# A hybrid mLSTM, attention and MoE layer: keys weighted on ScalarE as they leave PSUM, gate columns as bias of the exponential, late output transposes, wider adaLN sums

## The chip, the cores and the metric

The kernel runs on one core of a Trainium2 chip, in one launch. The metric is the device time of an execution in microseconds. Engines: PE is TensorE, DVE VectorE, ACT ScalarE, POOL GpSimd, SP the engine whose queue issues most DMAs.

## The reference, cut to what matters

One layer on 1024 tokens of width 1024, all in float32. The part that the change touches is the modulation (adaLN) and the mLSTM mixer with four heads of width 128, run forward and backward over the sequence. After it come dilated attention, the output projection and an expert-choice MoE with 16 experts, which the change leaves as they are.

```python
mod = jax.nn.silu(c) @ w_ada[l] + b_ada[l]          # 6 x 1024 numbers
shift1, scale1, gate1, shift2, scale2, gate2 = jnp.split(mod[:, None, :], 6, axis=-1)
h = rms_norm(x, norm1_g[l]) * (1.0 + scale1) + shift1
proj = h @ w_in[l]
x_m, o_pre, i_fw, f_fw, i_bw, f_bw, a_q, a_k, a_v = jnp.split(proj, split_points, axis=-1)
...
# mlstm_chunkwise, per head and direction (the kernel uses chunks of 128):
    w = jnp.exp(ac - m_new[..., None])               # weight of each key
    C_new = decay * C + einsum('bhl,bhld,bhle->bhde', w, kc, vc)
...
D = where(lower, b[..., :, None] - b[..., None, :] + i_pre[..., None, :], -inf)
w_intra = exp(D - m_t[..., None]) * einsum('bhcte,bhcje->bhctj', q, k)
num = w_inter[..., None] * einsum('bhcte,bhced->bhctd', q, C_prev) + einsum('bhctj,bhcjd->bhctd', w_intra, v)
h = num / maximum(abs(den), exp(-m_t))[..., None]
...
h = h_fwd + h_bwd
h = h * rsqrt(mean(h * h, -1) + 1e-6) * out_norm_g + skip * xc
```

## The kernel before, in words

The kernel is written in a tile language: Python says which instructions each part issues, and a list scheduler sorts them, by its own estimates, into one fixed order for each engine before anything runs. On the chip each engine follows its list and waits at an instruction until what it needs is there. The order views below are such lists.

The change lies in one stage, in which `body` interleaves three streams (`interleave((proj_stream, 1.0), (mlstm_stream, 1.9), (ada_stream, 1.0))`); the numbers that the streams yield are their estimated share of PE time, and steer in what order their work is handed to the scheduler.

- `proj_stream` computes the attention's q, k and v: 24 blocks of 128 tokens, 8 k-slabs and 3 products of 128x512 for each (lines L388, L389, L390), into the four PSUM buffers `pa`. ACT rounds each weight slab (`wh`, L345), DVE takes the rest (`wl`, L346), and DVE and ACT in turn move the results out (`ev`, L395, L397).
- `mlstm_stream` handles the gates first (`mlstm_gates`: scans over rows, which at L504 to L516 are transposed by PE, L513, into the columns `gcol`, or written to DRAM as `gate_rows_d`), then four heads one after another. A head: q by a product with a block diagonal matrix (L542, moved out by ACT, L543); the keys transposed (L552, moved out as `k` by ACT, L553); v (L557, L558); for each direction d the weights `W`, loaded as gate rows repeated over 128 partitions (POOL's DMA, L564), masked by POOL (L565), gate column added by DVE (L566), exponential by ACT (L567); `qw` loaded (L570) and multiplied with q (L573), its last columns copied by POOL as `dec` (L572); `kw`, the keys times a gate column, by POOL (L577). Then q·k on PE in two groups of four 128x128 (L583), multiplied into W by DVE (L586). Eight steps follow, each for both directions: state products (L600), intra-chunk and inter-chunk products (L605, L607), the state update on DVE (L613, L615), the denominators (L618 to L620) and the output (L624 on ACT, L626 on DVE). At the head's end the sum of squares (L629, L631), the inverse root (`rsqrt`, L134 to L139), the norm (L634), two groups of four transposes (L639), and the update of `og` (L641). The convolution of the next head (L523, L525) is issued within the head.
- `ada_stream` forms the upper 4096 numbers of `mod`: in 16 blocks of 256 columns, `w_ada` times silu(c) is summed on DVE over eight slabs (L319, L321 in `ada_sum`; SP's DMAs bring two slabs of 128x256 at once), then PE adds the 128 partitions with products by ones (L981), and DVE adds the bias (L982).

The last two streams share the four PSUM buffers `pb`. The tiles W, qw, kw and xc have two buffers each, q, k, v and h one; the square of L629 takes one of W's.

Of the kernel before, what the change touches and what calls it, by code (L numbers as in the profile page):

```python
# [20 lines left out]
P = 128  # L21
S = 1024
# [88 lines left out]
class K:  # L111
# [342 lines left out]
    def mlstm_gates(self):  # L454
# [30 lines left out]
        ch = lambda x: x.rearrange("p (c t) -> p c t", t=P)  # L485
        r_, c_, em, ws, wi = t, R("k"), R("q"), R("xc"), R("v")
        nc.vector.tensor_sub(r_, b_, m_)
# [41 lines left out]
    def mlstm_stream(self):  # L529
# [4 lines left out]
        self.mlstm_gates()  # L534
        yield 2.0
        for h in range(MH):
            xc, xm = xcs[h], self.xm[h]

            q = T("q")
            for b in range(2):  # L540
                ps = self.psB.tile([P, 512], F32, name="pb")
                nc.tensor.matmul(ps, self.amat[:, h, :], xc[:, b * 512:(b + 1) * 512], start=True, stop=True)  # L542
                nc.scalar.activation(q[:, b * 512:(b + 1) * 512], ps, AF.Copy)  # L543
            k = T("k", [P, NT, P])
            v = T("v", [P, NT, E1])
            nc.gpsimd.memset(v[:, :, P:E1], 1.0)
            yield 1.7
            for b in range(2):
                ps = self.psB.tile([P, 4, P], F32, name="pb")
                for i in range(4):  # L550
                    t = slice((4 * b + i) * P, (4 * b + i + 1) * P)
                    nc.tensor.transpose(ps[:, i, :], xc[:, t], self.ident)  # L552
                nc.scalar.activation(k[:, 4 * b:4 * b + 4, :], ps, AF.Copy)  # L553
                ps = self.psB.tile([P, 4, P], F32, name="pb")
                for i in range(4):
                    t0 = 2 + (4 * b + i) * P
                    nc.tensor.matmul(ps[:, i, :], xm[:, t0:t0 + P], self.bdv[:, h, :], start=True, stop=True)  # L557
                nc.scalar.activation(v[:, 4 * b:4 * b + 4, 0:P], ps, AF.Copy)  # L558
                yield 1.3

            W, QW_, KW, DEC = [], [], [], []
            for d in range(2):
                z = T("W", [P, NT, P])
                nc.gpsimd.dma_start(out=z, in_=bc(self.rows_d[0, d, h:h + 1, :], P))  # L564
                nc.gpsimd.tensor_add(z, z, self.mask[:, d:d + 1, :].to_broadcast([P, NT, P]))  # L565
                nc.vector.tensor_add(z, z, self.gcol[:, 0, :, MH * d + h][:, :, None].to_broadcast([P, NT, P]))  # L566
                nc.scalar.activation(z, z, AF.Exp)  # L567
                W.append(z)
                wi = T("qw")
                nc.gpsimd.dma_start(out=wi, in_=bc(self.rows_d[1, d, h:h + 1, :], P))  # L570
                dec = cw.tile([P, NT], F32, name="dec", bufs=4)
                nc.gpsimd.tensor_copy(dec, wi[:, P - 1:S:P] if d == 0 else wi[:, 0:S:P])  # L572
                nc.vector.tensor_mul(wi, wi, q)  # L573
                QW_.append(wi)
                DEC.append(dec)
                kw = T("kw", [P, NT, P])
                nc.gpsimd.tensor_mul(kw, k, self.gcol[:, 2, :, MH * d + h][:, :, None].to_broadcast([P, NT, P]))  # L577
                KW.append(kw)
            for b in range(2):
# [4 lines left out]
                for d in range(2):  # L584
                    w = W[d][:, 4 * b:4 * b + 4, :]
                    nc.vector.tensor_mul(w, w, ps)  # L586
                yield 0.9
            if h + 1 < MH:
                xcs[h + 1] = self.mlstm_conv(h + 1)
# [45 lines left out]
            yield 0.1  # L635
            for b in range(2):
                ps = self.psB.tile([P, 4, P], F32, name="pb")
                for i in range(4):
                    nc.tensor.transpose(ps[:, i, :], h_[:, 4 * b + i, :], self.ident)  # L639
                t = slice(b * 512, (b + 1) * 512)  # L640
                nc.vector.scalar_tensor_tensor(og[:, t], ps.rearrange("p a b -> p (a b)"), self.vcol("mlstm_norm_g", h), og[:, t], op0=OP.mult, op1=OP.add)  # L641
            yield 0.9

# [322 lines left out]
    def ada_stream(self):  # L966

        nc = self.nc
        wada = self.I["w_ada"].rearrange("(p k) n -> p k n", k=KT)
        for q in range(2 * KT):  # L970
            c = (KT + q) * 256
            acc = self.cw.tile([P, 256], F32, name="ada_acc2")
            for k in range(0, KT, 2):
                aw = self.cw.tile([P, 2, 256], F32, name="ada_w2", bufs=3)
                nc.sync.dma_start(out=aw, in_=wada[:, k:k + 2, c:c + 256])
                yield 0
                self.ada_sum(acc, aw, k)
                yield 1.5
            ps = self.psB.tile([P, 512], F32, name="pb")
            for j in range(2):  # L980
                nc.tensor.matmul(ps[:, j:j + 1], acc[:, j * P:(j + 1) * P], self.ones[:, 0:1], start=True, stop=True)  # L981
            nc.vector.tensor_add(self.modc[:, 2 * q:2 * q + 2], ps[:, 0:2], self.vcol("b_ada", 2 * KT + 2 * q, 2))  # L982
            yield 0.5

# [618 lines left out]
def body(tc, I, out):  # L1603
    with ExitStack() as ctx:
# [13 lines left out]
        k.cw = k.pool("mlstm_work", st_cw, side="right")  # L1618
        k.tags = dict(W=2, qw=2, kw=2, q=1, k=1, v=1, h=1, xc=2)
        interleave((k.proj_stream(), 1.0), (k.mlstm_stream(), 1.9), (k.ada_stream(), 1.0))  # L1620
# [81 lines left out]
```

## Time and profile before

| what | us |
|---|---|
| median of 3 runs | 1914.62 |
| the runs | 1909.89, 1918.05, 1914.62 |
| the profiled execution | 1909.63 |
| its span, first to last instruction | 1907.9 |
| mean granted PE clock over the span | 0.973 of full speed |

The profile comes from one execution. An engine is busy while an instruction runs; what ended an idle time is the wait that is named. A matmul with float32 operands shows as two instructions. "PEclk" is the clock that PE was granted, as a share of the full one. In the 40 slices of the span the stage described above is the third to the eighth: PE reads 9 8 9 8 9 8 there, POOL 1 3 2 1 2 1, the clock 9 8 9 9 9 9.

```profile
PE   6998989889998939999999999999999999999997
...
DVE  6778887668775787877877877877776777867765
ACT  4343231358774436766766765756766666666654
POOL 1313212122122000000100100100000001000000
PEclk9998999999999968999999999999999999999999
```

### The profile page before, as it was taken

Reading aid. Unit: us, or ns where it says so; the run is one execution under the profiler, and the core shown is the slowest. Engines: PE = TensorE matmul, PEld = TensorE weight load, DVE = VectorE, ACT = ScalarE, POOL = GpSimd, SP = SyncE. Lnnn points to the kernel's source line nnn. Section 1 sums busy time; section 2 is a strip of 40 time slices with the busy share of each in tenths; the row PEclk is TensorE's granted clock in tenths of the full one; section 3 lists DMA queues with packets and bytes.
Section 4 is the critical chain, followed back from the end, with each engine's and each line's share of the span. In section 5 each row is a group of like instructions: output and inputs, shape, how many; then the busy total and the mean of one; then the engine's idle time right before and its main releaser. Section 6 shows DMA issues by size and latency. Waiting matters only on the chain. (4 is left out here: it accounts for less than half of the span.)

```text
span 1907.9 us, 23733 instructions
## 1 busy us (share of the span) xinstructions
PE 1780.7 (93%) x8457; PEld 1383.5 (73%) x8457; DVE 1436.8 (75%) x2218; ACT 1096.5 (57%) x1429; POOL 221.5 (12%) x200
## 2 busy tenths in 40 slices
PE   6998989889998939999999999999999999999997
PEld 4677777778887837777777777776776777777775
DVE  6778887668775787877877877877776777867765
ACT  4343231358774436766766765756766666666654
POOL 1313212122122000000100100100000001000000
PEclk9998999999999968999999999999999999999999
DMA  9324565324656768999999999999999989999991
GB/s 262 94 85 150 178 198 158 86 61 98 137 135 147 281 252 303 348 345 399 348 348 390 361 343 386 348 345 349 366 352 364 349 344 369 343 353 339 335 367 33
DMA packets 172684, 517.35 MB, mean 271 GB/s; under 512 B 34615, under 2 KB 85175, under 8 KB 134935
## 3 DMA queue, kind: packets, MB, share of 16 engines
q1 hardware_dynamic: 157568, 482.07, 69.2%
q0 software_dynamic: 10208, 33.10, 6.9%
q10 hardware_dynamic: 4790, 0.68, 0.2%
q8 instruction: 66, 1.08, 0.2%
q14 instruction: 52, 0.42, 0.1%
HBM read 488.29 MB, written 27.50 MB: 270 GB/s over the span
## 5 line engine op out<-in xcount | busy, mean ns | idle before, releaser
L1462 DVE TENSOR_TENSOR wl<-w,wh 128x2048 fp32r<-128x2048 f32 x260 | 585.0, 2278 | 92.8 <-ACT wh L1461 92.2
L1461 ACT ACTIVATE wh<-w 128x2048 fp32r<-128x2048 f32 x260 | 492.3, 1913 | 180.5 <-PE py L1482 79.9
L1461 ACT ACTIVATE wh<-w_half 128x1024 fp32r<-128x1024 f32 x152 | 154.0, 1058 | 68.9 <-PE py L1482 34.9
L1462 DVE TENSOR_TENSOR wl<-w_half,wh 128x1024 fp32r<-128x1024 f32 x152 | 178.9, 1219 | 12.0 <-ACT wh L1461 11.8
L1482 PE MATMUL px<-wh,xTh 128*128 128x512 f32 x448 | 131.3, 411 | 2.1 <-ACT xTh L124 1.6
L1482 PE MATMUL py<-wh,xTh 128*128 128x512 f32 x448 | 131.3, 410 | 1.4 <-ACT wh L1461 1.2
L1482 PE MATMUL py<-wl,xTh 128*128 128x512 f32 x448 | 125.7, 400 | 5.6 <-DVE wl L1462 5.4
L1482 PE MATMUL px<-wl,xTh 128*128 128x512 f32 x448 | 125.9, 401 | 4.5 <-DVE wl L1462 4.5
L1482 PE MATMUL px<-wh,xTl 128*128 128x512 f32 x448 | 124.0, 397 | 0.0
L1482 PE MATMUL py<-wh,xTl 128*128 128x512 f32 x448 | 123.4, 395 | 0.0
L1541 POOL DMA_INDIRECT out_dram<-xin,idx x16 | 43.4, 2711 | 673.9 <-DVE xin L1540 673.9
L1482 PE MATMUL py<-wh,hT 128*128 128x512 f32 x448 | 118.1, 405 | 0.0
L1482 PE MATMUL px<-wh,hT 128*128 128x512 f32 x448 | 118.1, 405 | 0.0
L1482 PEld LDWEIGHTS px<-wl,xTh 128*128 128x128 f32 x448 | 83.4, 189 | 29.3 <-DVE wl L1462 9.5
L1482 PEld LDWEIGHTS py<-wl,xTh 128*128 128x128 f32 x448 | 82.6, 188 | 30.0 <-DVE wl L1462 11.3
L1482 PEld LDWEIGHTS px<-wh,xTh 128*128 128x128 f32 x448 | 83.1, 190 | 28.0 <-issue 6.7
L1482 PEld LDWEIGHTS py<-wh,xTh 128*128 128x128 f32 x448 | 82.9, 188 | 27.2 <-issue 7.7
L1482 PEld LDWEIGHTS px<-wh,hT 128*128 128x128 f32 x448 | 83.1, 188 | 22.8 <-issue 3.8
L1482 PEld LDWEIGHTS py<-wh,hT 128*128 128x128 f32 x448 | 83.0, 188 | 22.9 <-issue 3.8
L1482 PEld LDWEIGHTS px<-wh,xTl 128*128 128x128 f32 x448 | 84.7, 189 | 19.3
L1482 PEld LDWEIGHTS py<-wh,xTl 128*128 128x128 f32 x448 | 84.1, 188 | 19.1 <-DVE xTl L125 0.2
L321 DVE SCALAR_TENSOR_TENSOR ada_acc<-ada_w,silu_c,ada_acc 128x256 f32<-128x256 f32 x161 | 90.8, 575 | 6.1 <-DMA ada_w<-in_w_ada_dram 4.9
(460 smaller groups left out, 3413.5 us busy)
## 6 DMA issues: line engine op xcount, KB each, us to landing
w<-in_w_gate_dram SPq DMA_DIRECT2D x100, 1024.0 KB
w<-in_w_up_dram SPq DMA_DIRECT2D x96, 1024.0 KB
w<-in_w_down_dram SPq DMA_DIRECT2D x96, 1024.0 KB
w_half<-in_w_down_dram SPq DMA_DIRECT2D x62, 512.0 KB
w_half<-in_w_up_dram SPq DMA_DIRECT2D x58, 512.0 KB
w_half<-in_w_gate_dram SPq DMA_DIRECT2D x54, 512.0 KB
ada_w<-in_w_ada_dram SPq DMA_DIRECT2D x96, 256.0 KB
wraw<-in_w_in_dram SPq DMA_DIRECT2D x20, 512.0 KB
```

The lines of the kernel that those rows point to most:

```text
L321: nc.vector.scalar_tensor_tensor(acc, aw[:, j], self.sc[:, k:k + 1], acc, op0=OP.mult, op1=OP.add)
L1461: self.nc.scalar.activation(h[:, c], t, AF.Copy)
L1462: self.tc.keep_in_program_order(self.nc.vector.tensor_sub(l[:, c], t, h[:, c]))
L1482: nc.tensor.matmul(ps[c], x[:, t], y[o // m][:, o % m:o % m + 512], start=first and q == 0 and t == 0, stop=last and (q, t) == (len(prods) ...
L1541: nc.gpsimd.indirect_dma_start(out=self.out, out_offset=bass.IndirectOffsetOnAxis(ap=u["idx"][:, :1], axis=0), in_=y, in_offset=None, comp ...
```

## The change

Four things are done, all in the stage above (line numbers of the changed kernel stand from one to eleven higher).

- **Keys.** ACT no longer moves k out of PSUM whole. It writes `kw` of both directions straight from PSUM, 128x128 at a time, with the gate column as its scale (64 small activations in all). POOL's multiply is gone, as is the tile k; v gets two buffers.
- **Weights.** DVE adds the mask in place of POOL; the gate column is the bias of the exponential, which therefore goes in eight pieces of 128x128. ACT copies dec.
- **Output transposes.** The transposes of a head and the update of `og` become a generator, `mlstm_out`, whose two halves are issued behind the two q·k groups of the next head (of the last head at the end).
- **adaLN.** 8 blocks of 512 columns, one slab (128x512, 256 KB) for each DMA; the products with ones of a block are issued after two slabs of the next.

```diff
@@ -483,7 +483,7 @@
         nc.vector.tensor_tensor_scan(b_, sel, f, 0.0, OP.mult, OP.add)
         nc.vector.tensor_tensor_scan(m_, f, ig, 0.0, OP.add, OP.max)
         ch = lambda x: x.rearrange("p (c t) -> p c t", t=P)
-        r_, c_, em, ws, wi = t, R("k"), R("q"), R("xc"), R("v")
+        r_, c_, em, ws, wi = t, R("v"), R("q"), R("xc"), R("v")
         nc.vector.tensor_sub(r_, b_, m_)
         nc.vector.tensor_sub(c_, ig, b_)
         nc.scalar.activation(em, m_, AF.Exp, scale=-1.0)
@@ -533,6 +533,7 @@
         xcs = {0: self.mlstm_conv(0)}
         self.mlstm_gates()
         yield 2.0
+        last = None
         for h in range(MH):
             xc, xm = xcs[h], self.xm[h]
@@ -541,16 +542,19 @@
                 ps = self.psB.tile([P, 512], F32, name="pb")
                 nc.tensor.matmul(ps, self.amat[:, h, :], xc[:, b * 512:(b + 1) * 512], start=True, stop=True)
                 nc.scalar.activation(q[:, b * 512:(b + 1) * 512], ps, AF.Copy)
-            k = T("k", [P, NT, P])
             v = T("v", [P, NT, E1])
             nc.gpsimd.memset(v[:, :, P:E1], 1.0)
             yield 1.7
+            KW = [T("kw", [P, NT, P]) for d in range(2)]
             for b in range(2):
                 ps = self.psB.tile([P, 4, P], F32, name="pb")
                 for i in range(4):
                     t = slice((4 * b + i) * P, (4 * b + i + 1) * P)
                     nc.tensor.transpose(ps[:, i, :], xc[:, t], self.ident)
-                nc.scalar.activation(k[:, 4 * b:4 * b + 4, :], ps, AF.Copy)
+
+                for d in range(2):
+                    for i in range(4):
+                        nc.scalar.activation(KW[d][:, 4 * b + i, :], ps[:, i, :], AF.Copy, scale=self.gcol[:, 2, 4 * b + i, MH * d + h:MH * d + h + 1])
                 ps = self.psB.tile([P, 4, P], F32, name="pb")
                 for i in range(4):
                     t0 = 2 + (4 * b + i) * P
@@ -558,24 +562,21 @@
                 nc.scalar.activation(v[:, 4 * b:4 * b + 4, 0:P], ps, AF.Copy)
                 yield 1.3
-            W, QW_, KW, DEC = [], [], [], []
+            W, QW_, DEC = [], [], []
             for d in range(2):
                 z = T("W", [P, NT, P])
                 nc.gpsimd.dma_start(out=z, in_=bc(self.rows_d[0, d, h:h + 1, :], P))
-                nc.gpsimd.tensor_add(z, z, self.mask[:, d:d + 1, :].to_broadcast([P, NT, P]))
-                nc.vector.tensor_add(z, z, self.gcol[:, 0, :, MH * d + h][:, :, None].to_broadcast([P, NT, P]))
-                nc.scalar.activation(z, z, AF.Exp)
+                nc.vector.tensor_add(z, z, self.mask[:, d:d + 1, :].to_broadcast([P, NT, P]))
+                for c in range(NT):
+                    nc.scalar.activation(z[:, c, :], z[:, c, :], AF.Exp, bias=self.gcol[:, 0, c, MH * d + h:MH * d + h + 1])
                 W.append(z)
                 wi = T("qw")
                 nc.gpsimd.dma_start(out=wi, in_=bc(self.rows_d[1, d, h:h + 1, :], P))
                 dec = cw.tile([P, NT], F32, name="dec", bufs=4)
-                nc.gpsimd.tensor_copy(dec, wi[:, P - 1:S:P] if d == 0 else wi[:, 0:S:P])
+                nc.scalar.activation(dec, wi[:, P - 1:S:P] if d == 0 else wi[:, 0:S:P], AF.Copy)
                 nc.vector.tensor_mul(wi, wi, q)
                 QW_.append(wi)
                 DEC.append(dec)
-                kw = T("kw", [P, NT, P])
-                nc.gpsimd.tensor_mul(kw, k, self.gcol[:, 2, :, MH * d + h][:, :, None].to_broadcast([P, NT, P]))
-                KW.append(kw)
             for b in range(2):
                 ps = self.psB.tile([P, 4, P], F32, name="pb")
                 for i in range(4):
@@ -585,6 +586,8 @@
                     w = W[d][:, 4 * b:4 * b + 4, :]
                     nc.vector.tensor_mul(w, w, ps)
                 yield 0.9
+                if last:
+                    next(last)
             if h + 1 < MH:
                 xcs[h + 1] = self.mlstm_conv(h + 1)
             og = self.og[h]
@@ -633,13 +636,21 @@
             self.rsqrt(cw, rs, ss, P, "hn")
             nc.vector.tensor_mul(h_, h_, rs[:, :, None].to_broadcast([P, NT, P]))
             yield 0.1
-            for b in range(2):
-                ps = self.psB.tile([P, 4, P], F32, name="pb")
-                for i in range(4):
-                    nc.tensor.transpose(ps[:, i, :], h_[:, 4 * b + i, :], self.ident)
-                t = slice(b * 512, (b + 1) * 512)
-                nc.vector.scalar_tensor_tensor(og[:, t], ps.rearrange("p a b -> p (a b)"), self.vcol("mlstm_norm_g", h), og[:, t], op0=OP.mult, op1=OP.add)
-            yield 0.9
+            last = self.mlstm_out(h, h_, og)
+        for _ in range(2):
+            yield 2.6
+            next(last)
+
+    def mlstm_out(self, h, h_, og):
+
+        nc = self.nc
+        for b in range(2):
+            ps = self.psB.tile([P, 4, P], F32, name="pb")
+            for i in range(4):
+                nc.tensor.transpose(ps[:, i, :], h_[:, 4 * b + i, :], self.ident)
+            t = slice(b * 512, (b + 1) * 512)
+            nc.vector.scalar_tensor_tensor(og[:, t], ps.rearrange("p a b -> p (a b)"), self.vcol("mlstm_norm_g", h), og[:, t], op0=OP.mult, op1=OP.add)
+            yield
     def attn_tables(self):
@@ -967,20 +978,29 @@
         nc = self.nc
         wada = self.I["w_ada"].rearrange("(p k) n -> p k n", k=KT)
-        for q in range(2 * KT):
-            c = (KT + q) * 256
-            acc = self.cw.tile([P, 256], F32, name="ada_acc2")
-            for k in range(0, KT, 2):
-                aw = self.cw.tile([P, 2, 256], F32, name="ada_w2", bufs=3)
-                nc.sync.dma_start(out=aw, in_=wada[:, k:k + 2, c:c + 256])
+        def columns(q, acc):
+            ps = self.psB.tile([P, 512], F32, name="pb")
+            for j in range(4):
+                nc.tensor.matmul(ps[:, j:j + 1], acc[:, j * P:(j + 1) * P], self.ones[:, 0:1], start=True, stop=True)
+            nc.vector.tensor_add(self.modc[:, 4 * q:4 * q + 4], ps[:, 0:4], self.vcol("b_ada", 2 * KT + 4 * q, 4))
+
+        old = None
+        for q in range(KT):
+            c = (4 + q) * 512
+            acc = self.cw.tile([P, 512], F32, name="ada_acc2", bufs=2)
+            for k in range(KT):
+                aw = self.cw.tile([P, 1, 512], F32, name="ada_w2", bufs=3)
+                nc.sync.dma_start(out=aw, in_=wada[:, k:k + 1, c:c + 512])
                 yield 0
                 self.ada_sum(acc, aw, k)
                 yield 1.5
-            ps = self.psB.tile([P, 512], F32, name="pb")
-            for j in range(2):
-                nc.tensor.matmul(ps[:, j:j + 1], acc[:, j * P:(j + 1) * P], self.ones[:, 0:1], start=True, stop=True)
-            nc.vector.tensor_add(self.modc[:, 2 * q:2 * q + 2], ps[:, 0:2], self.vcol("b_ada", 2 * KT + 2 * q, 2))
-            yield 0.5
+
+                if k == 1 and old:
+                    columns(*old)
+                    yield 1.0
+            old = q, acc
+        yield 1.5
+        columns(*old)
     def ada_rows(self, pool, psum, c0, c1):
@@ -1616,7 +1636,7 @@
         k.qkv_d = tc.dram_tile([3, S, ML], F32, name="qkv_d")
         st_cw = ExitStack()
         k.cw = k.pool("mlstm_work", st_cw, side="right")
-        k.tags = dict(W=2, qw=2, kw=2, q=1, k=1, v=1, h=1, xc=2)
+        k.tags = dict(W=2, qw=2, kw=2, q=1, v=2, h=1, xc=2)
         interleave((k.proj_stream(), 1.0), (k.mlstm_stream(), 1.9), (k.ada_stream(), 1.0))
         st_cw.close()
         k.st_mp.close()
```

The scheduler turns this into new lists. Three places are shown; `m_W`, `m_kw`, `m_qw`, `m_v`, `m_h` are the tiles named above, `waits` names the engines or DMA queues whose signal the instruction waits for.

PE at head 0, before the first key products (L600, now L603): the list before.

```order
L557 MATMUL pb<-bdv,xm_831 128x128 x3
L583 MATMUL pb<-m_q,xc 128x128 [waits Activation_49]
L583 MATMUL pb<-m_q,xc 128x128 x3
L388 MATMUL pa<-wh,hTh 128x512
...
L389 MATMUL pa<-wl,hTh 128x512
L981 MATMUL pb<-ones,ada_acc_1126 128x1 [waits DVE_49,Activation_49]
L981 MATMUL pb<-ones,ada_acc_1126 128x1
L583 MATMUL pb<-m_q,xc 128x128 [waits Activation_49]
L583 MATMUL pb<-m_q,xc 128x128 x3
L600 MATMUL pb<-m_v,m_kw 128x129 [waits Activation_49,Pool_49]
```

And now:

```order
L561 MATMUL pb<-bdv,xm_831 128x128 x3
L584 MATMUL pb<-m_q,xc 128x128 [waits Activation_49]
L584 MATMUL pb<-m_q,xc 128x128 x3
L584 MATMUL pb<-m_q,xc 128x128 [waits Activation_49]
L584 MATMUL pb<-m_q,xc 128x128 x3
L390 MATMUL pa<-wh,hTl 128x512
L388 MATMUL pa<-wh,hTh 128x512
L389 MATMUL pa<-wl,hTh 128x512
L984 MATMUL pb<-ones,ada_acc_1067 128x1 [waits Activation_49]
L984 MATMUL pb<-ones,ada_acc_1067 128x1 x3
L390 MATMUL pa<-wh,hTl 128x512
L603 MATMUL pb<-m_v,m_kw 128x129 [waits Activation_49]
```

The second q·k group moved up to the first, and the key products wait for ACT alone. Of the sums' product, one block of 512 columns stands where one of 256 stood, and it no longer waits for DVE.

PE between two heads (0 and 1): the list before.

```order
L389 MATMUL pa<-wl,hTh 128x512
L639 MATMUL pb<-ident,m_h 128x128 [waits DVE_49,PE_49]
L639 MATMUL pb<-ident,m_h 128x128 x3
L639 MATMUL pb<-ident,m_h 128x128 [waits PE_49]
L639 MATMUL pb<-ident,m_h 128x128 x3
L542 MATMUL pb<-xc,amat 128x512 [waits PE_49]
L542 MATMUL pb<-xc,amat 128x512 [waits Activation_49]
L981 MATMUL pb<-ones,ada_acc_1545 128x1 [waits DVE_49]
L981 MATMUL pb<-ones,ada_acc_1545 128x1
L552 MATMUL pb<-ident,xc 128x128 [waits DVE_49]
```

And now, at the transposes of head 0:

```order
L388 MATMUL pa<-wh,hTh 128x512
L650 MATMUL pb<-ident,m_h 128x128 [waits DVE_49,PE_49]
L650 MATMUL pb<-ident,m_h 128x128 x3
L584 MATMUL pb<-m_q,xc 128x128 x4
L650 MATMUL pb<-ident,m_h 128x128 [waits PE_49]
L650 MATMUL pb<-ident,m_h 128x128 x3
L603 MATMUL pb<-m_v,m_kw 128x129 [waits DVE_49,PE_49,Pool_49]
L603 MATMUL pb<-m_v,m_kw 128x129
L389 MATMUL pa<-wl,hTh 128x512
```

The transposes (L639, now L650) stood ahead of everything of head 1. Now q, keys, values and the first q·k group of head 1 are ahead of them, and the key products right behind.

POOL in head 1: the list before.

```order
L564 DMA m_W<-gate_rows_d 128x1024 [waits DVE_49,Activation_49]
L564 DMA m_W<-gate_rows_d 128x1024 [waits DVE_49]
L565 TENSOR_TENSOR m_W<-m_W,mask 128x1024 [waits DMASW2_49]
L565 TENSOR_TENSOR m_W<-m_W,mask 128x1024 [waits DMASW3_49]
L577 TENSOR_TENSOR m_kw<-m_k,gcol 128x1024 [waits Activation_49]
L577 TENSOR_TENSOR m_kw<-m_k,gcol 128x1024
L570 DMA m_qw<-gate_rows_d 128x1024 [waits DVE_49,PE_49,Pool_49]
```

And now:

```order
L546 MEMSET m_v 128x8
L574 DMA m_qw<-gate_rows_d 128x1024 [waits PE_49] x2
L546 MEMSET m_v 128x8
L568 DMA m_W<-gate_rows_d 128x1024 [waits DVE_49] x2
L574 DMA m_qw<-gate_rows_d 128x1024 [waits DMASW4_49,PE_49,Activation_49]
```

Only loads and memsets are left on POOL, in this place and in the other heads.

## Rows read from the trace of the kernel before

**Rows 1.** The page: span, and busy time of each engine (share, instructions).

```profile
span 1907.9 us, 23733 instructions
...
PE 1780.7 (93%) x8457; PEld 1383.5 (73%) x8457; DVE 1436.8 (75%) x2218; ACT 1096.5 (57%) x1429; POOL 221.5 (12%) x200
```

**Rows 2.** Windows: stretch, length, busy PE, PEld, DVE, ACT, POOL, granted clock, DMA share, GB/s.

```profile
150.00:372.00 222.00, 192.54 (x1065) 163.48 (x1064) 176.07 (x402) 69.97 (x132) 49.20 (x43) 0.92 0.48 150
160.00:170.00 10.00, 3.64 (x18) 3.20 (x16) 8.84 (x8) 3.07 (x4) 5.46 (x3) 0.65 0.34 108
```

**Rows 3.** Waits of PE, 95 to 430 us: for whom, us in total, times, longest.

```profile
PE pb L981 <- DVE ada_acc L321: 11.1, 3, 6.4
PE pb L639 <- DVE m_h L634: 10.2, 4, 6.6
PE pb L513 <- DVE row_qw L504: 4.3, 1, 4.3
...
PE pa L388 <- ACT wh L345: 3.5, 1, 3.5
PE pb L600 <- POOL m_kw L577: 1.8, 2, 1.4
```

**Rows 4.** Timeline of PE: start, duration, line, operation, instructions joined, idle before.

```profile
160.11 0.40 PE L388 MATMUL pa<-wh,hTh 128*128 128x512 f32 x1
160.34 0.39 PE L389 MATMUL pa<-wl,hTh 128*128 128x512 f32 x1
167.09 0.98 PE L981 MATMUL pb<-ones,ada_acc 128*128 128x1 f32 x4 [6.36 <-DVE ada_acc L321]
...
171.07 0.63 PE L388 MATMUL pa<-wh,hTh 128*128 128x512 f32 x1
171.50 0.63 PE L389 MATMUL pa<-wl,hTh 128*128 128x512 f32 x1
```

**Rows 5.** Groups of DVE, 107 to 372 us: count, busy us, mean ns, idle before.

```profile
L321 DVE SCALAR_TENSOR_TENSOR ada_acc<-ada_w,silu_c,ada_acc 128x256 f32<-128x256 f32 x112 | 63.2, 565 | 5.8 <-DMA ada_w<-in_w_ada_dram 4.9
L525 DVE SCALAR_TENSOR_TENSOR xc<-xm,vcols,xc 128x1024 f32<-128x1024 f32 x16 | 20.4, 1277 | 0.1
...
L566 DVE TENSOR_TENSOR m_W<-m_W,gcol 128x1024 f32<-128x1024 f32 x8 | 14.1, 1763 | 5.5 <-POOL m_W L565 5.5
...
L319 DVE TENSOR_SCALAR ada_acc<-ada_w,silu_c 128x256 f32<-128x256 f32 x16 | 6.4, 403 | 0.0
...
L641 DVE SCALAR_TENSOR_TENSOR og<-pb,vcols,og 128x512 f32<-128x512 f32 x6 | 4.3, 746 | 0.3 <-PE pb L639 0.2
```

**Rows 6.** DVE lines L321 and L566, same stretch: ns minimum, median, maximum.

```profile
L321 DVE SCALAR_TENSOR_TENSOR ada_acc<-ada_w,silu_c,ada_acc x112: 461/479/2140, 118.1 to 329.7; 128x256 f32<-128x256 f32 x112
...
L566 DVE TENSOR_TENSOR m_W<-m_W,gcol x8: 1216/1222/3409, 160.0 to 339.1; 128x1024 f32<-128x1024 f32 x8
```

**Rows 7.** Timeline of POOL and DVE at 162 us.

```profile
162.24 2.89 POOL L577 TENSOR_TENSOR m_kw<-m_k,gcol 128x1024 f32<-128x1024 f32 x1
163.29 2.13 DVE L321 SCALAR_TENSOR_TENSOR ada_acc<-ada_w,silu_c,ada_acc 128x256 f32<-128x256 f32 x1
```

**Rows 8.** Groups of POOL, 107 to 372 us.

```profile
L565 POOL TENSOR_TENSOR m_W<-m_W,mask 128x1024 f32<-128x1024 f32 x8 | 19.8, 2477 | 9.1 <-DMA m_W<-gate_rows_d 9.1
L577 POOL TENSOR_TENSOR m_kw<-m_k,gcol 128x1024 f32<-128x1024 f32 x8 | 17.8, 2243 | 27.2 <-ACT m_k L553 27.2
```

**Rows 9.** Groups of ACT, 107 to 372 us.

```profile
L624 ACT ACTIVATE m_h<-pb,den 128x128 f32<-128x128 f32 x32 | 10.0, 364 | 9.3 <-DVE den L620 9.3
L567 ACT ACTIVATE m_W<-m_W 128x1024 f32<-128x1024 f32 x8 | 8.4, 1056 | 27.9 <-DVE m_W L566 27.5 <-DVE hn_y L139 0.4
...
L553 ACT ACTIVATE m_k<-pb 128x512 f32<-128x512 f32 x8 | 4.8, 597 | 1.4 <-PE pb L552 1.3
```

**Rows 10.** Timeline of ACT: two activations joined.

```profile
178.25 0.62 ACT L624 ACTIVATE m_h<-pb,den 128x128 f32<-128x128 f32 x2
```

**Rows 11.** ACT line L806, exponentials with a bias column: ns minimum, median, maximum.

```profile
L806 ACT ACTIVATE p<-p,stats x128: 438/497/514, 423.3 to 595.0; 128x256 f32<-128x256 f32 x112, 128x192 f32<-128x192 f32 x16
```

## The prediction

> **What bounds the kernel now.** I read the page first: TensorE (PE) is busy 93% of a span of 1907.9 us, VectorE (DVE) 75% [rows 1]. So the time is PE's work, its holes, and what it does at half clock. The change adds and removes no product: all 64 key transposes, 64 value products, the q·k products and the projections stay. What can change lies therefore in the holes and the clock of the one stage it touches, about 107 to 372 us; every other stage comes later by a shift.
>
> The windows view says what the stage has on offer [rows 2]. From 150 us on (mLSTM heads running) PE is busy 192.54 of 222 us: 29.5 us of holes. The granted clock there is 0.92 on average, so at most 0.08 x 222 = 17.8 us are lost to it. The loss is read in the second row, 160 to 170 us: PE works 3.64 of 10 us, the clock is 0.65. In the timeline [rows 4] two projection products stand 0.23 us apart before a hole (160.11, 160.34), and 0.43 apart behind it (171.07, 171.50): full speed, 2.4 GHz, and half, 1.2. Some of the low clock falls on idle time, where it costs nothing; I count 12 of the 17.8 as real. On offer: 29.5 + 12 = 41.5 us.
>
> The waits of PE say who makes the holes [rows 3]: the column sums of adaLN on DVE's accumulator 11.1 us, the output transposes on DVE's normalised h 10.2, the key products on POOL's kw 1.8. The change touches these three, 23.1 us. Two others, the gate columns (4.3) and a projection weight that comes from HBM over ACT (3.5), it leaves.
>
> **Why DVE is late there.** A 128x256 ada operation has a median of 479 ns and a longest of 2140; the gate-column add on the mask 1222 and 3409 [rows 6]. The long ones coincide with POOL arithmetic: at 163.29 an ada operation takes 2.13 us and ends as POOL's second kw multiply does (162.24 + 2.89) [rows 7]. Against the median the 112 ada operations (mean 565 [rows 5]) lose 112 x 0.086 = 9.6 us, the eight adds (mean 1763) 8 x 0.541 = 4.3: 13.9 us.
>
> The Trainium skill (*SBUF — State Buffer*, the section on two separate sides) calls the port pair that VectorE and GpSimd share an exclusive lock, whose loser is blocked for the other's whole instruction. The row at 163.29 agrees; the sum is no test of it, since 13.9 us is only what these two lines lost. By that rule DVE could win back up to all of POOL's 37.6 us, which speaks for the third rival below.
>
> **The parts.**
>
> *POOL's arithmetic goes.* Mask adds 19.8 us and kw multiplies 17.8 leave POOL [rows 8]; DVE gets back 13.9 by the rows, at the very most 37.6. The mask add goes to DVE in place of the gate-column add: eight 128x1024 operations for eight, nil. POOL is left with DMA issues and memsets, so the loads of W and qw wait for no arithmetic of its own any more; what they wait for is the free buffer, as before.
>
> *Wider ada sums.* 56 multiply-adds of 128x512 in place of 112 of 128x256. Between 479 ns at 256 columns and 1277 at 1024 [rows 5, 6] lies 745 at 512; the same form from PSUM at 512 takes 746. 112 x 0.479 = 53.6 against 56 x 0.745 = 41.7: 11.9 us less, and by the same ratio 1.4 less on the 16 first operations of the blocks (6.4 us now), which become 8. The number of DMAs is kept, 64 of 256 KB on SP, each with rows twice as long; priced at nothing, because the DMA share is 0.48 [rows 2] and three slabs are on the way ahead. The column products now stand behind two slabs of the next block, so they need a sum that is 1.5 us of DVE older. The two changes take 13.9 + 13.3 = 27 us off DVE's 176, about 7 per head.
>
> *ACT gets it.* A 128x128 activation from PSUM takes 364 ns, the second of a pair starting some 0.26 behind the first (two take 0.62) [rows 9, 10]. 64 kw activations: 17 to 23 us, against 4.8 for the eight k evacuations. Of an exponential of 128x128 with a bias column there is no row; nearest are 364 (128x128, scale column) and 497 (128x256, bias column) [rows 11]: 0.26 to 0.50. I take 0.30, nearer the first because the size is its own: 64 x 0.30 = 19 against 8.4 for eight of 128x1024 [rows 9]. Eight copies of dec add under 3. In all 21 to 45 us more on an engine that is busy 70 of 222 [rows 2]: room on average, none in a head's prologue, where q·k, W and kw are wanted at once. I price this within the holes below.
>
> *Late output transposes.* In the fixed order they stand behind the next head's first q·k group, with projection products ahead; DVE has a head's prologue more time for the norm. Their price: the first products of the head now wait behind them.
>
> **What holes stay.** Walking the new order with these durations: the gate columns 4.3 + 0.7 (three 512-wide ada operations, 3 x 0.745 = 2.2 us, now stand in DVE's gate chain; six projection products, 6 x 0.23 = 1.4 us, moved ahead of the wait) = 5.0, the late weight 3.5. Head 0: both q·k groups now follow the values with no projection between, so PE waits for ACT's evacuations and then for W: 4.5. From head 0 to 1 DVE has 20.7 us of work between the last state and the normalised h, PE 20 to fill it: 2.5 with the hand-overs. Head 1 to 2 (19.3 against 19): 1. Head 2 to 3 (12 against 19): 0. Inside the heads' loops 1.5. The gate wait lies ahead of 150 us, so only its growth of 0.7 counts here: 0.7 + 3.5 + 4.5 + 2.5 + 1 + 1.5 = 13.7 left of 29.5: **15.8 us less**. Of the 23.1 us of holes that the change touches 8 are left (4.5 + 2.5 + 1), a third, and I take the clock loss to shrink with them, to 4 of 12: **8 less**. Sum 24.
>
> The profiled execution took 1909.6 us (1.7 beside its span) and the median of the runs is 1914.6, 5 more. 1909.6 - 23.8 = 1885.8 against the profiled one; a median of several may lie 0 to 5 above that, and I say **1888**.
>
> **Rivals.**
>
> *Slower: ACT's small instructions become the wait.* Per head 16 kw (0.364) + 16 exponentials (0.497) + dec 0.6 = 14.4 us in place of 1.2 + 2.1 = 3.3 [rows 9]: 11 more, in the prologue, ahead of the first state products (kw) and intra-chunk products (W). If PE has nothing beside it: 44 us, 1909.6 - 24 + 44 = 1930. The point that decides is 6 us uncovered per head. For: at head 0 only five projection products (1.2 us) are left between q·k and the first key products, and evacuations of projections queue on ACT behind the exponentials. Against: before head 1 the order has 48 projection products between the second key group and the first product that takes a kw, 11 us of work beside which ACT can make them. I put it at 1925, chance 0.07.
>
> The Trainium skill (*ScalarE: Activation LUTs*, section "What ACT_TABLE_LOAD costs") gives an activation with a pointer operand about 280 ns fixed plus 0.833 a column, some 93 ns hidden back to back. That speaks against splitting one into eight: an estimate from it is 0.29 us each, close to the pair in [rows 10], and it leaves the sum where it is.
>
> *No change: the gaps only move.* DVE's seven free us per head are taken by other waits, for W after its exponentials or for the ada sums over the DMAs; the order before looked as tight on paper and had the holes all the same, so a walk by durations is optimistic. Half the DVE holes stay, and the new head 0 adds its 4.5: 1905 to 1912. Chance 0.14. That the transposes aren't late, or the ada products not moved, is not a case: the order shows both.
>
> *Nearly all closes.* If DVE wins back nearer to 37.6 than 13.9, each boundary has some 6 us to spare, and only the weight and head 0 stay: 1909.6 - 40 = 1868 to 1872. Chance 0.12.
>
> **How the numbers follow.** Forecast 0.67 (1875 to 1900), slower 0.07, no change 0.14, all closes 0.12. Two ends of the unknowns: exponentials at 0.50 add 13 us on ACT, of which I'd let half reach PE (1895); clock loss 17.8 all regained gives 1880. The range is 1868 to 1906, leaving out the slower rival, most of the no-change one and the tail of the third. About 0.5% (9.6 us) is what a measurement of this kernel can tell: faster is under 1905. Faster: 0.67 + 0.12 and little of the rest = 0.80; slower 0.07; same 0.13.
>
> **What would show it.** Right: no POOL arithmetic in the stage; ada operations at about 745 ns with none over 1.3 us; PE's waits on the ada sum and on the normalised h under 3 us together with a clock of about 0.97 in the stage; the last projection of the stage and everything behind it 24 us earlier. Wrong: PE waiting on ACT (kw, W) for more than 10 us in all; new waits on DVE of the old length; or ada operations no faster per column.

## The result, and the profile after

The changed kernel takes 1881.89 us (median of four executions, 1877.69 to 1884.02) beside 1912.26 us; the ratio is 0.9837, interval 0.9817 to 0.9857: 1.6% faster, about 31 us, where 1888 was forecast. The profiled execution took 1884.02 us. Its page, the lines that answer to [rows 1]:

```profile
span 1882.3 us, 23755 instructions
...
PE 1774.4 (94%) x8457; PEld 1380.5 (73%) x8457; DVE 1406.9 (75%) x2146; ACT 1119.4 (59%) x1549; POOL 182.6 (10%) x176
```

PE's products are the same in number. The stage, from the first L388 to the start of the last L390, shrank from 253.2 us (107.4 to 360.6) to 224.0 (111.1 to 335.1), by 29.2. It began 3.7 us later than in the profile before, in work that the change doesn't touch; over all profiles of this study that start lies between 107.4 and 114.0. So the table below gives lengths of the stage beside the times, and the spans of two profiles (25.6 us apart here) are compared only with care.

Windows of the changed kernel (length, busy PE, PEld, DVE, ACT, POOL, clock, DMA share, GB/s), 150 to 348 us, 24 us shorter than the window of before, and a slice in which the clock was low; they answer to [rows 2]:

```profile
150.00:348.00 198.00, 190.41 (x1107) 161.57 (x1106) 150.60 (x347) 97.65 (x256) 10.96 (x22) 0.98 0.55 175
...
200.00:210.00 10.00, 9.24 (x29) 7.42 (x30) 9.40 (x17) 7.54 (x20) 0.00 (x0) 0.67 0.71 226
```

PE stands 7.6 us of 198, where it stood 29.5 of 222, and the clock is 0.98 instead of 0.92. What is left is in its waits, which answer to [rows 3]:

```profile
PE pb L513 <- DVE row_qw L504: 4.0, 1, 4.0
PE pb L650 <- DVE m_h L637: 1.8, 1, 1.8
PE pa L389 <- DVE wl L346: 1.7, 1, 1.7
...
PE pb L608 <- DVE m_W L587: 1.3, 1, 1.3
PE pa L388 <- ACT wh L345: 1.2, 1, 1.2
```

The ada sums (11.1 us before) and kw are no longer waited for; for the normalised h PE waits 1.8 us instead of 10.2. DVE's and ACT's groups that answer to [rows 5, 9], 107 to 372 us:

```profile
L321 DVE SCALAR_TENSOR_TENSOR ada_acc<-ada_w,silu_c,ada_acc 128x512 f32<-128x512 f32 x56 | 41.8, 747 | 8.6 <-DMA ada_w<-in_w_ada_dram 8.5
...
L571 ACT ACTIVATE m_W<-m_W,gcol 128x128 f32<-128x128 f32 x64 | 19.9, 444 | 1.6 <-DVE m_W L569 1.5
L557 ACT ACTIVATE m_kw<-pb,gcol 128x128 f32<-128x128 f32 x64 | 17.4, 392 | 0.0
```

An ada operation takes 747 ns on the mean (745 forecast), and the longest of the stage 756, so none is long any more. The exponentials cost 19.9 us in all (19 forecast), the kw 17.4 (17 to 23).

### The profile page after: what moved, and what is told of

The parts are those of the page before. It is cut to its first block, busy times and chain, and to the rows that moved or that the text cites. A ratio compares the mean times of both kernels' runs of the same rounds, so it can differ in the third digit from the quotient of the medians.

```text
span 1882.3 us, 23755 instructions
## 1 busy us (share of the span) xinstructions
PE 1774.4 (94%) x8457; PEld 1380.5 (73%) x8457; DVE 1406.9 (75%) x2146; ACT 1119.4 (59%) x1549; POOL 182.6 (10%) x176
## 5 line engine op out<-in xcount | busy, mean ns | idle before, releaser
L1481 ACT ACTIVATE wh<-w 128x2048 fp32r<-128x2048 f32 x260 | 492.3, 1913 | 180.9 <-PE py L1502 80.7
L388 PE MATMUL pa<-wh,hTh 128*128 128x512 f32 x192 | 80.1, 418 | 1.3 <-ACT wh L345 1.2
```

Of the source, the lines that this page charges most:

```text
L388: nc.tensor.matmul(ps, hTh[:, k, t], hi[k], start=(k == 0), stop=False)
L1481: self.nc.scalar.activation(h[:, c], t, AF.Copy)
```

## The experiments

The change has three parts that can be taken one by one: **P** (POOL's arithmetic moved away: keys and weights), **T** (late transposes), **A** (the ada stream). Each was timed against the kernel before. "us" is the ratio less one, times 1913, with an interval of some 2 to 6 us to either side; "stage" is the length of the stage, as above, in the one profiled execution.

| parts | run | ratio (interval) | us | stage |
|---|---|---|---|---|
| none | before | 1 | 0 | 253.2 |
| T | e9 | 0.9991 (0.9978 to 1.0004) | -2 | 254.9 |
| A | e10 | 1.0035 (1.0022 to 1.0047) | +7 | 256.7 |
| T, A | e1 | 0.9949 (0.9932 to 0.9966) | -10 | 242.7 |
| P | e8 | 0.9880 (0.9863 to 0.9897) | -23 | 228.6 |
| P, A | e3 | 0.9886 (0.9859 to 0.9913) | -22 | 229.3 |
| P, T | e4 | 0.9896 (0.9870 to 0.9922) | -20 | 235.2 |
| P, T, A | the change | 0.9837 (0.9817 to 0.9857) | -31 | 224.0 |
| weights, T, A | e6 | 0.9851 (0.9835 to 0.9868) | -28 | 235.4 |
| keys, T, A | e7 | 0.9907 (0.9892 to 0.9923) | -18 | 237.4 |
| P, T, A, idle POOL work, short | e2 | 0.9867 (0.9835 to 0.9899) | -25 | 232.0 |
| P, T, A, idle POOL work, long | e5 | 0.9928 (0.9912 to 0.9944) | -14 | 242.5 |
| P, T, A, columns at once | e11 | 0.9830 (0.9809 to 0.9850) | -33 | 221.6 |
| P, T, A, ada later | e12 | 0.9803 (0.9783 to 0.9823) | -38 | 217.6 |

**POOL's parts undone (e1).**

```diff
-    nc.scalar.activation(KW[d][:, 4 * b + i, :], ps[:, i, :], AF.Copy, scale=self.gcol[...])
+ nc.scalar.activation(k[:, 4 * b:4 * b + 4, :], ps, AF.Copy)
+ nc.gpsimd.tensor_mul(kw, k, self.gcol[...].to_broadcast([P, NT, P]))
...
+ nc.gpsimd.tensor_add(z, z, self.mask[...].to_broadcast([P, NT, P]))
```

> The changed kernel with both POOL parts undone: POOL again adds the mask, multiplies kw and copies dec, ACT moves k out whole and takes the exponential in one piece; the late transposes and the wider ada sums stay. My theory (DVE's relief, of which the end of contention with POOL is about half, and the later places close the holes together): about half of the 30 us come back, 12 us slower than the changed kernel (1894), with ada operations of over 1.5 us among the 56 again. Rival 'the places alone': at most 3 us slower (1885). Rival 'contention alone': nearly all comes back, 20 or more (1902 or more).

1903.28 us, 21 lost: more than my 12, and what the rival 'contention alone' had named. The ada operations and the gate-column add of e1:

```profile
L321 DVE SCALAR_TENSOR_TENSOR ada_acc<-ada_w,silu_c,ada_acc 128x512 f32<-128x512 f32 x56 | 51.7, 924 | 5.7 <-DMA ada_w<-in_w_ada_dram 5.6
L567 DVE TENSOR_TENSOR m_W<-m_W,gcol 128x1024 f32<-128x1024 f32 x8 | 15.2, 1913 | 2.4 <-POOL m_W L566 2.4
```

Against the changed kernel 56 x 0.177 = 9.9 and 8 x 0.69 = 5.5 us more; the tiny steps of the inverse root (L137 to L139) add 8.7: DVE lost 24 us. Is it this, or the waits for POOL's results (PE on kw 4.3 us here)? Two kernels add work on POOL that nobody waits for.

**Idle work on POOL, short (e2) and long (e5).** e2 adds 64 instructions of 128x256 (the expectation says 128; the columns it gives are right), e5 16 of 128x1024, whose scratch tile takes one of v's two buffers. In the traces of both, PE, DVE and ACT run the stage's instructions in the same order as in the changed kernel, so that POOL's work and that buffer are all that differs:

```diff
  QW_.append(wi)
+ for r in range(8):                                    # e2
+     m = KW[d][:, 2 * (r % 4):2 * (r % 4) + 2, :]
+     nc.gpsimd.tensor_mul(scr, m, m)
...
+ nc.gpsimd.tensor_add(scr, KW[d], self.mask[...].to_broadcast([P, NT, P]))     # e5
+ nc.gpsimd.tensor_mul(scr, KW[d], self.gcol[...].to_broadcast([P, NT, P]))
```

> The changed kernel with 128 throwaway multiplies of 128x256 on POOL added (each reads two chunks of a kw and writes a scratch tile that nobody reads, as many columns as POOL's two steps handled before); nothing else changes and the output is the same. It has POOL's arithmetic without anyone waiting for its results. My theory: DVE's long operations return, about 14 us of them, and some 6 us reach the end (1888). Rival 'contention alone': 14 or more (1896). Rival 'the wait for POOL's results was the cost, not the contention': within 2 us of the changed kernel.

> Like the second experiment, but the throwaway work has the form of POOL's steps before: for each head and direction one addition with the mask and one multiply with the gate column, 128x1024 each, on kw, into a tile that nobody reads (it takes the place of one of v's two buffers, so the gates' rows lie as before). 16 instructions of some 2.3 us. The first experiment showed 21 us for undoing POOL's parts and 24 us of longer DVE operations; the second only 8 us of longer operations and 5 us of time. Theory A (the length of POOL's instructions decides how long DVE stands): DVE operations lose 20 us or more and the time rises by 12 to 20 (1894 to 1902). Theory B (waiting for POOL's results costs most of the 21): as the second experiment, 3 to 7 us (1885 to 1889).

e2 took 1886.90 us, e5 1901.40. e5's groups of DVE, ACT and POOL, 107 to 372 us:

```profile
L321 DVE SCALAR_TENSOR_TENSOR ada_acc<-ada_w,silu_c,ada_acc 128x512 f32<-128x512 f32 x56 | 47.3, 845 | 5.7 <-DMA ada_w<-in_w_ada_dram 5.5
...
L580 POOL TENSOR_TENSOR m_k<-m_kw,mask 128x1024 f32<-128x1024 f32 x8 | 21.8, 2724 | 25.6 <-ACT m_kw L557 25.3
...
L581 POOL TENSOR_TENSOR m_k<-m_kw,gcol 128x1024 f32<-128x1024 f32 x8 | 17.8, 2231 | 0.6
L557 ACT ACTIVATE m_kw<-pb,gcol 128x128 f32<-128x128 f32 x64 | 17.4, 393 | 0.0
...
L139 DVE SCALAR_TENSOR_TENSOR hn_y<-hn_t,hn_y 128x8 f32<-128x8 f32 x8 | 6.9, 867 | 0.1
...
L138 DVE SCALAR_TENSOR_TENSOR hn_t<-hn_t,hn_v 128x8 f32<-128x8 f32 x12 | 6.2, 519 | 0.2
```

Rows of its timeline, at 167, 172 and 211 us:

```profile
167.61 1.92 POOL L581 TENSOR_TENSOR m_k<-m_kw,gcol 128x1024 f32<-128x1024 f32 x1
167.76 2.31 DVE L321 SCALAR_TENSOR_TENSOR ada_acc<-ada_w,silu_c,ada_acc 128x512 f32<-128x512 f32 x1 [2.47 <-DMA ada_w<-in_w_ada_dram]
...
172.35 2.24 POOL L581 TENSOR_TENSOR m_k<-m_kw,gcol 128x1024 f32<-128x1024 f32 x1
...
173.15 0.67 DVE L590 TENSOR_TENSOR m_W<-m_W,pb 128x512 f32<-128x512 f32 x1
...
210.61 3.29 POOL L580 TENSOR_TENSOR m_k<-m_kw,mask 128x1024 f32<-128x1024 f32 x1
...
211.62 2.31 DVE L138 SCALAR_TENSOR_TENSOR hn_t<-hn_t,hn_v 128x8 f32<-128x8 f32 x1
```

An operation of 128x8, which takes 0.16 us alone, has a mean of up to 0.87: the one at 211.62 stands until POOL's instruction ends (213.90) and itself ends at 213.93. So does the ada operation at 167.76, which ends 0.54 us behind POOL's. Not every DVE operation does: of those that began while one of the 16 POOL instructions ran, the eleven with all operands in SBUF stood, and the ten that read PSUM kept their length, as the product with `pb` at 173.15. Summed over these groups DVE lost 19 us in e5, and the kernel 17. ACT's kw writes had no idle time ahead of them and the mask adds only 0.6 us, so neither POOL's late release of kw nor its late loads explain it, and ACT's writes of v had none either (0.0), so it isn't v's lost buffer: theory A. PE's waits in e5, 95 to 430 us, show the way to the end:

```profile
PE pb L653 <- DVE m_h L640: 9.8, 2, 9.2
PE pa L389 <- DVE wl L346: 7.2, 2, 5.8
PE pb L611 <- DVE m_W L590: 4.2, 1, 4.2
```

In the changed kernel these three are 1.8, 1.7 and 1.3: 16.4 us more, beside the 17 that the kernel lost. In e2 POOL was busy longer (61.7 us), but by the same sum DVE lost only 8 (10 with every group counted) and the kernel 6, with an interval that overlaps the change's; its stage is 8 us longer (groups of DVE and POOL in e2):

```profile
L321 DVE SCALAR_TENSOR_TENSOR ada_acc<-ada_w,silu_c,ada_acc 128x512 f32<-128x512 f32 x56 | 42.8, 764 | 7.8 <-DMA ada_w<-in_w_ada_dram 7.5
...
L582 POOL TENSOR_TENSOR scr<-m_kw 128x256 f32<-128x256 f32 x64 | 61.7, 965 | 22.5 <-ACT m_kw L557 18.1
```

A DVE operation that stood lost at most 0.45 us in e2, and up to 2.2 in e5. Length is the likely reason, though the operands differ too (the same tile twice, against a tile and a repeated mask or column), and that was not tried apart.

The Trainium skill (*SBUF — State Buffer*, the section on two separate sides) says that the loser of the port pair that VectorE and GpSimd share is blocked for the other's whole instruction; the row at 167.76 agrees. That DVE would lose all of POOL's time doesn't follow: 19 of 39.6 us.

**Keys or weights alone back on POOL (e6, e7).** The edits are the two halves of e1's.

> The changed kernel with the keys' part alone undone: ACT moves k out whole, POOL multiplies kw (8 instructions); the weights stay on DVE and ACT. Theory A: half of POOL's long instructions, half of the 21 us: 10 us slower (1892). Theory B: the key products wait for POOL, 4 us as in the first experiment, and little else: 5 us (1887). A gain would show that ACT's 64 small activations cost more than POOL's work.

> The changed kernel with the weights' part alone undone: POOL adds the mask and copies dec, DVE adds the gate column, ACT takes the exponential in one piece of 128x1024. Theory A: half of the 21 us, 10 slower (1892). Theory B: W is late behind POOL and a second step, in the prologue of each head: 14 slower or more (1896), with PE's waits on W or, through DVE's list, on the normalised h.

1886.63 and 1896.26 us: by the times the keys are worth 3 (their interval overlaps the change's), the weights 13. By the stage it is 11 and 13: the profiled execution of e6 lost 11.4 us in the stage and won some 7 back outside it, so what the keys are worth, 3 to 11, stays open. Theory A's 10 for each is therefore not borne out by the times, and e7 came out near theory B, with the wait for the normalised h that it named. DVE lost 8 us in e6 and 12 in e7, by the same sum; in e7 the stretched add also stands in the chain of W, and PE waited 9.1 us for the normalised h, 3.1 for the ada sum. Over e6, e2, e7, e5 and e1 DVE's losses of 8, 8, 12, 19 and 24 us go with 3, 6, 13, 17 and 21 in time; but in e1, e6 and e7 the scheduler's order on PE, DVE and ACT differs from the changed kernel's in many places, so only e2 and e5 show the contention alone.

**Parts alone, and transposes or ada undone (e8, e9, e10, e3, e4).** Each takes the lines of the diff above that belong to its parts, no others.

> The kernel before with the keys' and the weights' parts of the change, but its early transposes and narrow ada sums. If the parts add up, this gains what the first experiment lost, 21 us (1892 beside 1913). My theory: DVE's relief alone leaves the places early, so the waits on the ada sum and the normalised h shrink to half: 12 us faster (1901). Rival 'the relief pays only together with the later places': within 5 us of the kernel before.

> The kernel before with the late output transposes alone. The first experiment showed that the late transposes and the wider sums together, with POOL as before, are worth 10 us; beside POOL's relief neither of the two showed a gain without the other (third and fourth experiment, 1892 and 1894, beside 1890 with POOL's parts alone). Theory (a hole closes only when every late thing on DVE is out of PE's way; closing one leaves the next): within 5 us of the kernel before, with the wait for the normalised h smaller and the one for the ada sum larger. Rival 'the parts add': 5 to 10 us faster, half of the 10 at least.

> The kernel before with the wider ada sums and their later column products alone. Theory (closing one hole leaves the next): within 5 us of the kernel before, PE's wait for the ada sum gone and the waits for the normalised h and POOL's kw larger. Rival 'the parts add': 5 to 10 us faster. Rival 'DVE's work counts': the sums save 13 us of DVE, so 8 or more.

> The changed kernel with the output transposes back at the end of their own head, the rest as changed. My theory: PE waits again for the normalised h at three heads, 3 us or so each less what DVE's relief covers, and the clock falls behind the longer ones: 6 us slower (1888). Rival 'the places alone': the wait is back in full, 10.2 us and its clock, 13 us slower (1895). Rival 'contention alone': within 2 us.

> The changed kernel with the ada stream of before (16 blocks of 256 columns, products with ones right behind the last sum). My theory: DVE gets 13 us of work back and the column products are early again; PE waits for the ada sum some 5 us in all and loses clock behind it: 8 us slower (1890). Rival 'the places alone': 11 us of waits and the clock, 14 us slower (1896). Rival 'contention alone': within 3 us.

Medians: 1890.00, 1910.18, 1921.14, 1891.96, 1893.78. P alone brings 23 of the 31 us, twice the 12 that I gave it; undoing T or A (e3, e4) costs 9 and 11, where 6 and 8 were expected. T and A are worth nothing or less alone, beside P or not, and 8 to 10 together. The waits tell where the time went. With T alone (e9) the transposes are never late, and the ada columns (L992, before L981) take over:

```profile
PE pb L992 <- DVE ada_acc L321: 22.7, 4, 6.5
```

With A alone (e10) it is the other way round, and worse than before. The wait for the ada sum is gone, that for the normalised h is as it was (10.2), and results of the projection, kw, weights and W are waited for instead:

```profile
PE pb L639 <- DVE m_h L634: 10.3, 3, 9.7
PE pa L388 <- DVE ev L395: 6.9, 1, 6.9
PE pb L600 <- POOL m_kw L577: 5.8, 4, 2.4
PE pa L389 <- DVE wl L346: 5.1, 2, 3.2
...
PE pb L605 <- DVE m_W L586: 3.5, 2, 1.9
```

Wider sums lengthen the chain on DVE between a head's sum of squares and its norm. In e8 (narrow) and then in e3 (wide), both with early transposes, head 0:

```profile
199.85 1.21 DVE L631 TENSOR_REDUCE ss<-m_W 128x8 f32<-128x1024 f32 x1
...
209.18 1.22 DVE L634 TENSOR_TENSOR m_h<-m_h,rs 128x1024 f32<-128x1024 f32 x1
```

```profile
193.39 1.22 DVE L632 TENSOR_REDUCE ss<-m_W 128x8 f32<-128x1024 f32 x1
...
210.38 1.21 DVE L635 TENSOR_TENSOR m_h<-m_h,rs 128x1024 f32<-128x1024 f32 x1
```

10.6 us from the first to the end of the second with two ada operations (1.0 us) between; 18.2 with six (4.2 us), loads and weight roundings that this order put there as well. At head 1 it is 14.2 and 18.2. Early transposes wait for that chain, but for little of it: PE's waits for the normalised h in e8, then in e3, are

```profile
PE pb L639 <- DVE m_h L634: 5.3, 3, 3.3
```

```profile
PE pb L640 <- DVE m_h L635: 5.6, 3, 5.1
```

So the longer chain can explain that wider sums don't shorten this wait, not the 7 us that e10 lost; where those come from beyond the waits above stays open. In the changed kernel the chain is as long (18.2 at head 0), and nobody waits for it there.

**Width or place of the ada sums (e11).**

```diff
-                if k == 1 and old:
-                    columns(*old)
-                    yield 1.0
+            columns(q, acc)
```

> The changed kernel with the wider ada sums, but the products with ones issued right behind the last sum of their block instead of two slabs later. It splits the ada part in two: if the width (13 us less DVE work) is what counts, within 3 us of the changed kernel (1882 to 1885); if the place counts, 6 to 12 slower (1888 to 1894), with PE waiting for the ada sum.

1880.57 us: the place is worth nothing, though PE did wait once, 5.4 us, for an ada sum, as the rival had it. So what e4 lost (11 us) is the width. How much of that is DVE's 13 us and how much the longer rows of the loads stays open.

**A try at a better kernel (e12).**

```diff
         old = None
+        yield 20.0
         for q in range(KT):
```

> The changed kernel with the ada stream's share of the work started 20 us later by the streams' own count, so that its sums and loads spread over the heads (by the order 20, 38 and 56 of the 64 sums precede the norms of heads 0, 1 and 2, instead of 28, 48 and 64). A try at a better kernel: DVE has more than half of its time free at the end of the stage, and the loads of a projection weight, W and the ada slabs collide at 190 to 200 us. If that collision makes the remaining holes: 3 to 5 us faster than the changed kernel (1877 to 1879). If the holes are DVE's chains in the heads' ends: no difference within 3 us.

1874.13 us (1870.92 to 1880.25): 38 us less than before, 6 to 8 less than the change, though the two intervals touch (0.9817 to 0.9823). The stage took 217.6 us (108.3 to 325.9) instead of 224.0. Its window, and PE's waits for weights, 95 to 400 us:

```profile
150.00:342.00 192.00, 186.79 (x1109) 159.57 (x1108) 151.57 (x346) 93.00 (x252) 9.63 (x19) 1.00 0.58 184
```

```profile
PE pa L389 <- DVE wl L346: 0.8, 1, 0.8
...
PE pa L388 <- ACT wh L345: 0.6, 1, 0.6
```

PE stands 5.2 us instead of 7.6, and is busy 3.6 us less for as many products. The waits for weights fell from 2.9 to 1.4 us, and the full clock came back: in the changed kernel two such waits stood side by side, and products behind them ran at half clock:

```profile
198.55 0.50 PE L388 MATMUL pa<-wh,hTh 128*128 128x512 f32 x1 [1.18 <-ACT wh L345]
200.76 0.80 PE L389 MATMUL pa<-wl,hTh 128*128 128x512 f32 x1 [1.71 <-DVE wl L346]
201.35 0.63 PE L390 MATMUL pa<-wh,hTl 128*128 128x512 f32 x1
201.78 0.63 PE L388 MATMUL pa<-wh,hTh 128*128 128x512 f32 x1
```

0.43 us apart, 1.2 GHz, in a slice at 0.67 (above); that slice alone lost up to 3.3 us. That the later start takes the ada loads out of the weights' way fits this, but it moves DVE's order too, and the two were not tried apart.

## Why the prediction was right, point by point

- *What bounds the stage.* Right. Holes and clock were on offer, 41.5 us; the stage gave back 29.2 of them, 24 were forecast. The signs it named came: no wait for the ada sum and 1.8 us for the normalised h, a clock of 0.98, the last L390 25.5 us earlier. Too cautious were the holes left and what DVE gets back from POOL, both below. (The profile has 32 key transposes and not 64; nothing was worked out from that.)
- *"DVE gets back 13.9 by the rows."* The mechanism was right (e5), the term too small. It counted two lines; L137 and L138, nine each in the stretch of [rows 5], had means of 395 and 406 ns instead of 0.16 us, 4 us more, and in the order of e1 POOL costs DVE 24. And before e1 and e8 I put P at about half of the gain; alone it has three quarters (e8). The forecast was added up from the holes of the whole order and not from the parts, so this wrong share didn't reach its number; that is luck as far as the parts go.
- *Wider sums, 13.3 us less on DVE.* Right in size: 41.8 + 3.8 us now, 59 before at the undisturbed durations. That it pays only with the late transposes, and costs 7 us alone, the prediction didn't say.
- *ACT.* 19.9 + 17.4 us, inside the range. The slower rival falls: PE waited for neither kw nor, on ACT, for W. The estimate from the Trainium skill (*ScalarE: Activation LUTs*, "What ACT_TABLE_LOAD costs") was 0.29 us each; the exponentials took 19.9 / 64 = 0.31, the kw 0.27.
- *Holes left, 13.7 us.* 7.6 measured. Head 0 cost 1.3 instead of 4.5: there ACT was busy 9.98 us between 160 and 170 us, but PE had work (8.64). Head 0 to 1 had no wait for h (2.5 forecast), head 1 to 2 1.8 (1), the weights 2.9 (3.5), the gates 4.0 (5.0).
- *Clock, 4 of 12 us left.* At most (1 - 0.98) x 198 = 4.0 are.
- *Rivals.* "The gaps only move" is what T and A do alone (e9, e10); it was the wrong case for the whole, of which P alone brings 23 us. At 1882 the result lies between the forecast (1888) and "nearly all closes" (1868 to 1872); e12, at 1874, comes nearer to the latter.

## What to carry to other kernels

In this kernel POOL's arithmetic had a second price beside its own time: VectorE instructions with all operands in SBUF that started beside a long POOL instruction stood until it ended, and those that read PSUM did not. Where VectorE feeds the critical engine, much of that loss can reach the end: 17 of 19 us in e5, 6 of 8 in e2. Price it by comparing mean and median of VectorE's groups, the tiny ones too. Parts that each move one late product may only shift the hole to the next one, as T and A did alone; test them together before discarding one.

## What was not expected of the hardware

A VectorE operation of 0.16 us had a mean of 0.87 in the kernel with 16 POOL instructions of 2.2 to 2.7 us whose results nobody reads (e5), while operations that read PSUM lost nothing beside the same instructions, and 64 POOL instructions of 0.97 us (e2) cost VectorE less than half as much (8 us against 19).
